# A two-layer decoder trunk on one core: the opening's products of c on 128 rows, four modulations moved to ScalarE, other durations in the instruction planner

## The chip, the cores and the metric

The kernel runs on one core of a Trainium2 chip. The time is that of one execution on the device in microseconds (us). Differences are told by several executions of each kernel on the same chip; the profile is that of one more execution. PE is TensorE (its weight loads are shown as PEld), DVE is VectorE, ACT is ScalarE, POOL is GpSimd and SP is SyncE, which issues most transfers.

## The reference

The kernel computes a decoder trunk of two layers on 256 tokens of width 1024, in float32. Each layer is a half feed-forward step, a token mixer and another half feed-forward step. Each sub-layer normalizes x and modulates it with a shift, a scale and a gate that come from a vector c:

```python
c_act = silu(c)
for layer in range(2):
    sh1, sc1, g1, sh2, sc2, g2, sh3, sc3, g3 = split(c_act @ ada_w[layer] + ada_b[layer], 9)
    h = modulate(rms_norm(x, norm_g[layer, 0]), sh1, sc1)          # h * (1 + sc) + sh
    x = x + 0.5 * g1 * swiglu(h, w_gate[layer, 0], w_up[layer, 0], w_down[layer, 0])   # 1024 -> 2816 -> 1024
    h = modulate(rms_norm(x, norm_g[layer, 1]), sh2, sc2)
    mix = moba_attention(h, ...) if layer == 0 else mla_attention(h, ..., shared_k, shared_v)
    x = x + g2 * mix
    h = modulate(rms_norm(x, norm_g[layer, 2]), sh3, sc3)
    x = x + 0.5 * g3 * swiglu(h, w_gate[layer, 1], w_up[layer, 1], w_down[layer, 1])
```

The second layer's mixer (MLA) makes its queries through a latent of 384 columns, and its shared keys and values through a latent of 256 columns, from x normalized and modulated a second time with a shift and scale of their own (`kv`). There are 16 heads of 64 + 32 columns.

## The kernel before

*Products.* A product of float32 accuracy is made of three: each operand is split into a high part of reduced precision (fp32r) and the rest, and PE adds hi x hi, lo x hi and hi x lo (L774 to L776; in the feed-forward's down-projections and elsewhere L979 and L987). Weights stream in through SP's queue into three raw buffers; ACT rounds them (hi, L644) and DVE subtracts (lo, L645). Activations that leave PSUM are split likewise: ACT hi (L789), DVE lo (L790). The score and value products of the attention (L1043, L1048, L1103) are whole float32 products, with the mask added by a bf16 product (L1044). Transposes are made on PE (L824, L1083, L1410, L1475).

*Who sets the order.* The program is written with delays between its parts, but what stands in each engine's queue in the end is set by a planner (class `Order`). It records every instruction, gives each a duration by a formula (`duration()`, L205 to L250), adds costs such as `SWITCH` for PE's passing to a slow float32 product, places the instructions of every engine one after another with a priority by what is due when, several times over, keeps the best plan, and fixes this order on every engine. A change of a duration formula so reorders instructions of all engines anywhere in the program, without any of them being other work. Instructions inside `ranked(n)` are placed early, in order of n.

*The opening* (`first()`). c is loaded as 32 rows of 256, runs through Silu on ACT twice (L1562 rounded, L1563 whole) and is split. Eight products with a column of the identity broadcast as weights (`row_r`, L1568, 32 rows) spread c over all 128 partitions, four from the high part and four from the rest, into two PSUM tiles; ACT copies them to `c_b` (L1571, two copies of 512 columns). The adaLN columns of the first norm are then made on DVE, for each of 8 steps k: two products with c_b summed along the row (L655, 1024 columns each, for shift and scale), then the scale becomes (1 + scale) x gain (`scale_col`, L660). x is transposed on PE together with its normalization (L1603; from k = 2 on, ACT normalizes, L1607, and PE transposes, L1608). ACT modulates (z, L1620, 256 columns), and z is split into h (ACT L789, DVE L790). The first feed-forward weights of each step are rounded and split (whi, ACT L1631; wlo, DVE L1632) as they land, and 36 products (L1640 to L1642) add into six PSUM accumulators. These are opened by products of zeros (L1579): one each, and two for the accumulators 1 to 3, nine in all; ten more (L1610) fill the wait after the first transposes.

*The second mixer's entry.* When a row tile t of x (128 rows; there are two) is done, `norm_T` and `modulate_cols` make four pieces of 256 columns (c0 = 0, 256, 512, 768): ACT scales x by its norm (y, L819), PE transposes two blocks (L824), and each block is modulated for the mixer's own h and for the `kv` path. The `kv` modulations (z) are on DVE (L840); those of h are on ACT (L842), but those with c0 of 512 and more, where there are two uses, are on DVE too. `split_h` then splits each. `mla()` follows with the latent products of both tiles (L774 to L776, with 384 columns for queries and 288 for keys and values), the latents' norm (L1400 to L1405), their transposes and splits (qlT and ckT, L1410, L789, L790), the up-projections, the head norms and rotations, and four groups of heads: scores, mask, maximum (DVE L1057), exponentials (ACT L1068), transposes of the result (L1083, copied by ACT L1085) and value products (L1103).

## Time and profile before

| what | us |
|---|---|
| median of three executions | 994.26 |
| lowest and highest | 993.56, 994.35 |
| the profiled execution, its own time | 993.19 |
| its span in the profile | 990.8 |

The profiled execution's mean TensorE clock was 0.999 of full speed. A row of a single engine's timeline gives the start, the time, the engine, the line, the operation, what it writes and reads, shapes and a count of neighbours of one kind, and in brackets how long the engine was idle before it and what ended this. A matmul's time in these rows reaches from its start to its end and overlaps with the next one's; the distance of two starts is what one costs. A line such as L1640 is one of the kernel before.

### The profile page before, as it was taken

What the parts mean: (1) busy time and instruction counts of PE and PEld (TensorE: products, weight loads), DVE (VectorE), ACT (ScalarE), POOL (GpSimd) and SP (SyncE); (2) the same over time, 40 slices, a digit from 0 to 9 for tenths busy, and PEclk for the clock granted to TensorE, in tenths of its full rate; (3) what the DMA queues carried; (4) which work ended last, traced back from release to release, by engine and by line L of the source; (5) the groups of instructions that cost most, each with busy time, mean ns of one, the idle gap of its engine ahead of it and who ended that gap; (6) DMA issues with size and microseconds to landing.
All of it is one profiled execution on the core that took longest, in us unless ns stands there. A gap on an engine that the chain in (4) does not pass through costs nothing.

```text
span 990.8 us, 15241 instructions
## 1 busy us (share of the span) xinstructions
PE 979.4 (99%) x5565; PEld 832.1 (84%) x5565; DVE 845.8 (85%) x1431; ACT 629.2 (64%) x1176; POOL 85.6 (9%) x120
## 2 busy tenths in 40 slices
PE   8999999999999999999999999999999999999998
PEld 7988888888887788888888888888888878888886
DVE  7999999898999899999798999974899789677542
ACT  5699565378666966555377665633869796666421
POOL 1012100022131000000010000000143110000000
PEclk9999999999999999999999999999999999999999
DMA  9978989898777678989889988872333568545630
GB/s 367 409 268 280 348 304 370 290 362 304 270 282 259 240 291 317 324 305 347 299 312 323 329 315 335 286 287 88 107 112 128 213 241 300 182 170 175 228 128 21
DMA packets 53274, 260.55 MB, mean 263 GB/s; under 512 B 6192, under 2 KB 6736, under 8 KB 35024
## 3 DMA queue, kind: packets, MB, share of 16 engines
q1 hardware_dynamic: 51696, 255.93, 70.8%
q0 software_dynamic: 1024, 3.17, 1.1%
q8 instruction: 43, 0.70, 0.3%
q10 hardware_dynamic: 480, 0.49, 0.2%
q14 instruction: 31, 0.25, 0.1%
HBM read 255.37 MB, written 4.19 MB: 262 GB/s over the span
## 4 chain that ended last, share of the span: by engine, by line
PE 93%; DVE 3%; DMA 2%; ACT 1%; issue 1%; POOL 0%; ACTq 0%; SPq 0%
PE mm L979 26%; PE mm L774 15%; PE mm L775 15%; PE mm L776 15%; PE mm L987 13%; DMA raw<-in_first_dram 2%; PE at L1103 1%; PE at L1083 1%; PE at L1043 1%; PE tr L1204 1%; PE tr L824 1%; PE tr L1475 1%; PE at L1048 1%; DVE wlo L1632 1%; DVE adaw L655 1%
## 5 line engine op out<-in xcount | busy, mean ns | idle before, releaser
L645 DVE TENSOR_TENSOR lo<-raw,hi 128x1024 fp32r<-128x1024 f32 (+3 forms) x312 | 369.7, 1200 | 69.2 <-ACT hi L644 63.7
L644 ACT ACTIVATE hi<-raw 128x1024 fp32r<-128x1024 f32 (+3 forms) x312 | 320.8, 1038 | 152.5 <-PE mm L776 115.9
L979 PE MATMUL mm<-h,hi 128*128 128x512 f32 x1120 | 288.6, 394 | 0.0
L979 PEld LDWEIGHTS mm<-h,hi 128*128 128x128 f32 x1120 | 199.6, 189 | 34.4
L987 PEld LDWEIGHTS mm<-h,lo 128*128 128x128 f32 x1120 | 155.5, 190 | 12.1
L987 PE MATMUL mm<-h,lo 128*128 128x256 f32 x1120 | 162.3, 283 | 0.0
L655 DVE CUSTOM_DVE_ANT_0 adaw<-adaw,c_b,cols 128x1024 f32<-128x1024 f32 x112 | 141.5, 1278 | 3.0 <-ACT c_b L1571 1.8
L774 PE MATMUL mm<-hi,gh 128*128 128x512 f32 x352 | 137.5, 390 | 0.0
L775 PE MATMUL mm<-lo,gh 128*128 128x512 f32 x352 | 137.2, 390 | 0.0
L776 PE MATMUL mm<-hi,gl 128*128 128x512 f32 x352 | 137.2, 390 | 0.0
L774 PE MATMUL mm<-hi,h 128*128 128x512 f32 (+1 forms) x240 | 95.2, 401 | 0.4 <-ACT h L789 0.3
L776 PE MATMUL mm<-hi,h 128*128 128x512 f32 (+1 forms) x240 | 92.6, 392 | 1.0 <-DVE h L790 1.0
L775 PE MATMUL mm<-lo,h 128*128 128x512 f32 (+1 forms) x240 | 93.0, 391 | 0.0
L776 PEld LDWEIGHTS mm<-hi,gl 128*128 128x128 f32 x352 | 66.1, 188 | 13.9
L775 PEld LDWEIGHTS mm<-lo,gh 128*128 128x128 f32 x352 | 66.1, 188 | 13.3
L774 PEld LDWEIGHTS mm<-hi,gh 128*128 128x128 f32 x352 | 66.1, 188 | 13.3
L693 DVE SCALAR_TENSOR_TENSOR acc<-adaw,cols,acc 128x1024 f32<-128x1024 f32 x48 | 61.3, 1278 | 0.2
L774 PEld LDWEIGHTS mm<-hi,h 128*128 128x128 f32 x240 | 45.1, 188 | 10.2 <-issue 1.3
L776 PEld LDWEIGHTS mm<-hi,h 128*128 128x128 f32 x240 | 45.1, 188 | 10.1 <-DVE h L790 1.2
L775 PEld LDWEIGHTS mm<-lo,h 128*128 128x128 f32 x240 | 45.2, 188 | 7.8
L811 POOL TENSOR_TENSOR rstd<-ssq,mhalf 128x1 f32<-128x1 f32 x12 | 13.5, 1125 | 411.0 <-DVE ssq L806 344.0
L916 ACT ACTIVATE u<-mm 128x256 f32<-128x256 f32 x70 | 26.4, 377 | 34.8 <-PE mm L987 33.6
(240 smaller groups left out, 1246.7 us busy)
## 6 DMA issues: line engine op xcount, KB each, us to landing
raw<-in_w_dram SPq DMA_DIRECT2D x142, 1024.0 KB, 5.4
adaw<-in_ada_dram SPq DMA_DIRECT2D x160, 512.0 KB, 5.5
raw<-in_w_dram SPq DMA_DIRECT2D x12, 512.0 KB, 3.5
raw<-in_first_dram SPq DMA_DIRECT2D x7, 512.0 KB, 9.0
raw<-in_w_dram SPq DMA_DIRECT2D x6, 576.0 KB, 3.7
bias_d<-bt SPq DMA_DIRECT2D x12, 256.0 KB, 3.9
bg<-bias_d POOLq DMA_DIRECT2D x4, 768.0 KB, 6.2
raw<-in_first_dram SPq DMA_DIRECT2D x10, 256.0 KB, 9.0
```

What stands on the lines that cost most here:

```text
L644: nc.scalar.activation(hi, src, AF.Copy)
L645: nc.vector.tensor_tensor(lo, src, hi.bitcast(F32), op=ALU.subtract)
L655: nc.vector.tensor_tensor_reduce(wt, wt, c_b, 1.0, cols[:, i, c:c + 1], op0=ALU.mult, op1=ALU.add, accum_out=m_cols[:, i, c:c + 1])
L693: nc.vector.scalar_tensor_tensor(acc, ada_tile(j, k), cact[:, k:k + 1], acc, op0=ALU.mult, op1=ALU.add)
L774: nc.tensor.matmul(ps, lh, rh, start=start, stop=False)
L775: nc.tensor.matmul(ps, lh, rl, start=False, stop=False)
L776: nc.tensor.matmul(ps, ll, rh, start=False, stop=stop)
L811: nc.gpsimd.tensor_tensor(r, stats[t], mhalf[:, 0:1], op=ALU.pow)
L824: nc.tensor.transpose(kslice(pt, j), kslice(y, j), ident)
L916: nc.scalar.activation(x, ps[:, S:], AF.Copy)
L979: nc.tensor.matmul(ps[i], w[0], hs[2], start=k == 0, stop=False)
L987: nc.tensor.matmul(ps[i][:, S:], w, hk_, start=False, stop=k == KD - 1)
```

## The change

It has three parts.

1. *The planner's figures.* A DVE tensor_scalar with two pointer operands (the modulation) is given 267 + 1.05 n ns instead of 205 + 0.54 n. PE's change of kind is given 95 into a float32 product, 140 (`BACK`) out of one, and -80 (`T_TO_R`) from a transpose to another product. A chain that keeps neighbouring value products together holds the products of c together as well.
2. *The opening.* c's two parts are whole tiles of 128 rows whose rows 32 to 127 are cleared by four memsets on DVE; `row_r` has 128 rows, so c's products run over 128 rows. c's transfer is issued first. One half of `c_b` is copied by ACT, the other by DVE. The accumulators 1 to 3 are opened by four products of zeros each instead of two (15 in all). The scale becomes (1 + scale) x gain on ACT (one column, Identity with scale and bias) and no longer on DVE. In step 0, ACT writes h's high part straight from the transposed x, DVE writes z from it as well, and DVE subtracts; the other steps keep z on ACT and the split.
3. *The second mixer's entry.* For the second row tile (t = 1) the modulations of h with c0 of 512 and more go to ACT: four of 128 columns.

```diff
+BACK = 140.0
+T_TO_R = -80.0
...
+            elif len(aps) > 3 and not full:
+                d = 267.0 + 1.05 * n if n > 8 else d
...
-            half = type(i).__name__ == "InstMatmult" and aps[0].ap[0][1] == DH
+            half = type(i).__name__ == "InstMatmult" and (aps[0].ap[0][1] == DH or aps[1].ap[-1][0] == 0)
...
-                slow = self.ins[k].ins[0].dtype == F32 and not self.ins[k].is_transpose
-                if slow and not dtype:
-                    occ, dur = occ + SWITCH, dur + SWITCH
-                dtype = slow
+                kind = ("transpose" if self.ins[k].is_transpose else
+                        "slow" if self.ins[k].ins[0].dtype == F32 else "product")
+                d = (SWITCH if kind == "slow" and dtype != "slow" else 0.0 if kind == "slow" else
+                     BACK if dtype == "slow" else
+                     T_TO_R if dtype == "transpose" and kind == "product" else 0.0)
+                occ, dur = occ + d, dur + d
+                dtype = kind
...
-                    modulate(pt[:, c:c + step], z[:, c:c + step], key, (c0 + c) // P, step,
-                             on_vector=i > 0 or len(keys) > 1 and c0 >= 512)
+                    modulate(pt[:, c:c + step], z[:, c:c + step], key, (c0 + c) // P, P,
+                             on_vector=i > 0 or len(keys) > 1 and t == 0 and c0 >= 512)
...
-            c4, chi, clo = [tp.tile([P, S], x, tag="y", name=nm("c"), bufs=4)[:32] for x in (F32, F32R, F32R)]
-            row_r = fp.tile([32, 4], F32R, name="row_r")
-            nc.vector.tensor_copy(row_r, ident[:32, :4])
+            c4, chi, clo = [tp.tile([P, S], x, tag="y", name=nm("c"), bufs=4) for x in (F32, F32R, F32R)]
+            with ranked(0):
+                nc.scalar.dma_start(c4[:32], a["c"])
+                for x in (chi, clo):
+                    for p in (32, 64):
+                        nc.vector.memset(x[p:2 * p].bitcast(F32), 0.0)
+            row_r = fp.tile([P, 4], F32R, name="row_r")
+            nc.vector.tensor_copy(row_r, ident[:, :4])
...
-                for i in range(2):
-                    nc.scalar.activation(c_b[:, i * 512:(i + 1) * 512], pc[i], AF.Copy)
+                nc.scalar.activation(c_b[:, :512], pc[0], AF.Copy)
+                nc.vector.tensor_copy(c_b[:, 512:], pc[1])
...
-                for i in range(2 if 1 <= f < 4 else 1):
+                for i in range(4 if 1 <= f < 4 else 1):
...
-                    scale_col(key, k, 1)
+                    g = col_slice(2, key, k, 1)
+                    nc.scalar.activation(col_slice(1, key, k, 1), col_slice(1, key, k, 1), AF.Identity, scale=g, bias=g)
...
-                    nc.scalar.activation(z, xT[k], AF.Identity, scale=col_slice(1, key, k, 1), bias=col_slice(0, key, k, 1))
...
-                    split_evac(hh, hl, z)
+                    if k:
+                        modulate(xT[k], z, key, k, S)
+                        split_evac(hh, hl, z)
+                    else:
+                        modulate(xT[k], hh, key, k, S)
+                        modulate(xT[k], z, key, k, S, on_vector=True)
+                        nc.vector.tensor_tensor(hl, z, hh.bitcast(F32), op=ALU.subtract)
```

The queues of SP and POOL keep their order. PE's, DVE's and ACT's change in some sixty stretches, since the planner sees other costs; most of them lie in the opening, in the mixers (207 to 360 and 699 to 819 us of the profile before) and at 514 to 531 us.

More of the change, by code (lines that the diff above doesn't have):

```diff
@@ L836, in modulate @@
     def modulate(xT, z, key, k0, n, on_vector=False):
-        for j in range(n // P):
+        for j in range(xT.shape[-1] // n):
+            js = slice(j * n, (j + 1) * n)
             shift, scale = [col_slice(i, key, k0 + j, 1) for i in range(2)]
             if on_vector:
-                nc.vector.tensor_scalar(kslice(z, j), kslice(xT, j), scale, shift, op0=ALU.mult, op1=ALU.add)
+                nc.vector.tensor_scalar(z[:, js], xT[:, js], scale, shift, op0=ALU.mult, op1=ALU.add)
             else:
-                nc.scalar.activation(kslice(z, j), kslice(xT, j), AF.Identity,
-                        scale=scale, bias=shift)
+                nc.scalar.activation(z[:, js], xT[:, js], AF.Identity, scale=scale, bias=shift)
     def split_h(h, c0, n, z):
```

9 lines of the change are left out of this document (4 added, 5 removed).

## The prediction

> **What bounds the kernel now.** I read the page first, then the chain of waits for the opening, then what PE waits for around the second mixer's entry, and last the rows of single engines there.
>
> ```profile
> span 990.8 us, 15241 instructions
> ...
> PE 979.4 (99%) x5565; PEld 832.1 (84%) x5565; DVE 845.8 (85%) x1431; ACT 629.2 (64%) x1176; POOL 85.6 (9%) x120
> ...
> PE 93%; DVE 3%; DMA 2%; ACT 1%; issue 1%; POOL 0%; ACTq 0%; SPq 0%
> ```
>
> PE sets the end: 93% of the chain. The change takes away no product of the layers, so it can only win where PE waits: in the opening (the chain's share of DVE, DMA and ACT), and at the second mixer's entry. The time of this profiled execution is 993.19 us, 1.07 below the median of 994.26; I make the sum as a difference against the profiled execution and add it to the median.
>
> The chain of waits over the first 60 us (start, length, what) shows the opening:
>
> ```profile
> 44.80 0.57 ACT z L1620
> 45.40 0.43 ACT h L789
> ```
>
> From 45.83 on (45.40 and 0.43) PE has all it needs of the first layer, so whatever the opening wins must show as an earlier z of the last of its eight steps.
>
> What PE waits for from 695 to 735 us (total, times, longest):
>
> ```profile
> PE mm L776 <- DVE h L790: 1.0, 1, 1.0
> PE mm L774 <- ACT ckT L789: 0.8, 1, 0.8
> PE mm L774 <- ACT qlT L789: 0.6, 1, 0.6
> PE mm L776 <- DVE qlT L790: 0.3, 1, 0.3
> PE mm L775 <- DVE lo L645: 0.2, 1, 0.2
> ```
>
> These five waits are 2.9 us of idle time. A wait costs PE some 0.2 more than that, because products else overlap (by 0.16: 787.88 and 0.40 against 788.12, in the rows under (e)) and the first one behind it is slow; so 3.9 us is all that the second part can win there. The stretches in which they lie (columns: window, length, busy PE, PEld, DVE, ACT, POOL with counts, clock, DMA share, GB/s):
>
> ```profile
> 700.00:710.00 10.00, 8.85 (x55) 8.04 (x54) 9.73 (x26) 8.64 (x24) 1.00 (x1) 1.00 0.34 101
> 710.00:720.00 10.00, 9.58 (x62) 8.68 (x61) 9.55 (x28) 7.55 (x23) 3.25 (x4) 1.00 0.13 47
> 740.00:750.00 10.00, 10.00 (x81) 8.27 (x80) 9.58 (x21) 9.23 (x28) 2.59 (x2) 1.00 0.41 140
> ```
>
> DVE is the full engine there (9.73 of 10), but ACT has only 1.36 us free in the first stretch and 2.45 in the second.
>
> **Part one, the opening.** The rows of ACT, DVE and PE (start, length, line, what, count, idle before and its releaser):
>
> ```profile
> 6.61 1.08 ACT L1571 ACTIVATE c_b<-tr 128x512 f32<-128x512 f32 x2 [2.20 <-PE tr L1568]
> ...
> 43.05 1.59 ACT L1631 ACTIVATE whi<-raw 128x1024 fp32r<-128x1024 f32 x2 [1.82 <-DMA raw<-in_first_dram]
> 44.80 0.56 ACT L1620 ACTIVATE z<-tr,m_cols 128x256 f32<-128x256 f32 x1 [0.16 <-DVE m_cols L660]
> ```
> ```profile
> 7.80 1.28 DVE L655 CUSTOM_DVE_ANT_0 adaw<-adaw,c_b,cols 128x1024 f32<-128x1024 f32 x1 [1.80 <-ACT c_b L1571]
> ...
> 44.62 0.15 DVE L660 SCALAR_TENSOR_TENSOR m_cols<-m_cols,cols 128x1 f32<-128x1 f32 x1
> ```
> ```profile
> 1.00 3.17 PE L1579 MATMUL mm<-zeros 128*128 128x512 bf16 x7 [1.00 <-DVE zeros L1528]
> 4.09 1.22 PE L1568 MATMUL tr<-c,row_r 32*128 32x256 f32 x4
> ```
>
> ```profile
> 0.83 0.11 DVE L1528 MEMSET zeros<- 128x64 uint32 x1 [0.83 <-PEq L1682]
> ...
> 0.93 0.17 DVE L619 MEMSET ones_r<- 128x128 f32 x1
> ```
>
> *Head.* Of the four new memsets three stand on DVE ahead of the one that clears zeros, which PE waits for until 1.00. They clear 256 columns each; the nearest row clears 128 in 0.17, so I take 0.2 us each, 0.6 in all (bounds 0 and 1). Then seven zeros products of 3.17 us end near 4.75 instead of 4.17, and the products of c start some 0.55 later than 4.09. Their price of 1.22 for four is kept: the columns streamed are the same. Against that, one zeros product that stood between the two halves of c's products (0.5 us) moves behind them, and the second copy of c_b goes to DVE: the two copies take 1.08 one after the other, so side by side half of it, 0.5, goes. Sum: +0.6 - 0.5 - 0.5, with a wait between engines more; the first column of DVE starts at 7.8 or up to half a us earlier. The six more zeros products (6 x 0.45 = 2.7 us at the pitch of the seven) stand behind c's products, where PE waits for x and c_b in any case until 9.31.
>
> *Body and end.* What is won at the head doesn't reach the end. The last raw tile lands at 43.03 (whi waits 1.82 us for it and starts at 43.05); ACT then rounds it in two pieces of 1.59 us together, to 44.64; z stands behind these and starts at 44.80, 0.16 later, because the scale L660 on DVE ends at 44.77. If L660 goes, z can start at 44.64 at the earliest, unless it is put ahead of the rounding; but the step that takes its place on ACT (one column, some 0.1 between neighbours) stands in the same row behind the first piece. In the changed order ACT does: one piece, the scale, the other piece, z, h. So z starts at 44.70 to 44.75. **Value: -0.1 us**, bounds 0 (the scale costs ACT what DVE saved) and -0.16. Only if the transfers land earlier could it be more, and their order on SP is unchanged:
>
> ```profile
> 30.00:40.00 10.00, 9.93 (x85) 9.72 (x84) 10.00 (x17) 6.87 (x12) 0.00 (x0) 1.00 1.03 405
> ```
>
> the DMA engines are full (1.03) at 405 GB/s, so an earlier free buffer brings no tile sooner. The first step's side by side h (ACT) and z (DVE) saves one pass of some 0.5 us there, at 11 us, well ahead of these landings: nothing at the end.
>
> *A page on the 128 rows.* The seven zeros products are 0.45 us apart for 512 columns, while products of that width are 0.24 apart later (788.12 after 787.88 below): PE begins at half its rate although the clock column says 1.00. The Trainium skill, page "TensorE: Matmul & The Clock Gate", section "Part 1: The HAM clock gate", has PE at half rate until a window of about 3.4 us was busy; the section "Why this matters for your kernels" says that a single product on 32 rows takes the time of one on 128. By the second, 128 rows win nothing in themselves; by the first, an unbroken run of full products could end the half rate earlier, which would halve the 2.4 us of c's products at most. The trace shows no case of this, and by the landing at 43.03 the end would stand all the same.
>
> **Part two, the second mixer's entry.**
>
> ```profile
> 700.59 0.72 DVE L840 TENSOR_SCALAR y<-tr,m_cols 128x128 f32<-128x128 f32 x2
> 701.23 0.41 DVE L790 TENSOR_TENSOR h<-y,h 128x256 fp32r<-128x256 f32 x1
> ...
> 702.68 1.36 DVE L840 TENSOR_SCALAR z<-tr,m_cols 128x128 f32<-128x128 f32 x4
> 703.96 1.04 DVE L645 TENSOR_TENSOR lo<-raw,hi 128x864 fp32r<-128x864 f32 x1
> ```
> ```profile
> 701.70 0.44 PE L776 MATMUL mm<-hi,h 128*128 128x384 f32 x1 [0.96 <-DVE h L790]
> ...
> 705.06 0.40 PE L775 MATMUL mm<-lo,hkv 128*128 128x288 f32 x1 [0.18 <-DVE lo L645]
> ```
> ```profile
> L842 ACT ACTIVATE y<-tr,m_cols x72: 433/447/462, 208.1 to 813.0; 128x128 f32<-128x128 f32 x72
> ```
>
> DVE's modulations come 0.32 us apart (four from 702.68 to 703.96). The four that move are those of the second row tile (c0 of 512 and more): 4 x 0.32 = 1.28 us less on DVE, and 4 x 0.4 = 1.6 us more on ACT (0.447 each alone, less when pipelined).
>
> (a) They lie behind 705, so the *first* wait isn't touched by them; but the new durations reorder DVE. Between the residual's end and the split that PE waits for at 701.70 stand three modulations instead of two, one more at 0.32: **+0.3**.
>
> (b) The split lo of the kv weights (703.96, PE waits for it at 705.06) goes behind six z modulations and a split of hkv, at (a)'s 0.3 later, and ends near 706.2 instead of 705.0. PE resumes there at 706.3: **+1.2** in all, (a) among it. Two transposes of y, which wait for y of L819 and so for a split of hkv, stand at the same place.
>
> (c) From there DVE is 1.28 us lighter, and the second tile's h comes at some 706.4 instead of 707.0. The later waits, for qlT (0.6 and 0.3) and ckT (0.8), cost 1.7 + 3 x 0.2 = 2.3, and I take them as gone: +1.2 - 2.3 = -1.1 near 725. Behind that, the weight split for the next products has DVE's column of moved splits ahead of it; I take half of its 1.04 us as a new wait, which leaves **0.5 us ahead** at 733. The bounds of (b) and (c) together are -3.9 (no wait left) and +1.2 (the later waits stay).
>
> (d) What follows takes it back. The attention's first scores stand behind this, and their exponentials fill ACT:
>
> ```profile
> 738.42 0.37 ACT L1068 ACTIVATE s<-at,mx 128x128 f32<-128x128 f32 x1 [1.35 <-DVE mx L1057]
> ...
> 743.88 1.59 ACT L1085 ACTIVATE pT<-at 128x512 f32<-128x512 f32 x3
> ```
>
> ACT runs almost without a pause from 738.42 to 745.4 (9.23 busy of the 10 us from 740), and PE's transposes wait for it. In the new order the first mask product comes behind one score more (0.43 us), so it is 0.5 - 0.43 = 0.07 earlier: of the 0.5 us ahead, 0.07 is left at 745.
>
> (e) PE's order is changed in many places, since the planner's prices of switches differ. Whether a switch costs is seen here:
>
> ```profile
> 785.47 0.63 PE L774 MATMUL mm<-hi,h 128*128 128x512 f32 x2
> 786.03 1.58 PE L1103 MATMUL at<-pT,v 128*64 128x128 f32 x24
> 787.54 0.50 PE L776 MATMUL mm<-hi,h 128*128 128x512 f32 x1
> 787.88 0.40 PE L774 MATMUL mm<-hi,h 128*128 128x512 f32 x1
> 788.12 0.40 PE L775 MATMUL mm<-lo,h 128*128 128x512 f32 x1
> ```
> ```profile
> 779.26 0.39 PE L774 MATMUL mm<-hi,h 128*128 128x512 f32 x1
> 779.49 1.03 PE L1043 MATMUL at<-kT,qT 96*128 96x256 f32 x4
> 780.36 0.27 PE L1044 MATMUL at<-mask,ident_b 128*128 128x256 bf16 x1
> ```
>
> Out of the products with 64 wide weights (L1103) the first follower takes 0.34 instead of 0.24 (787.54 to 787.88), and into them there is the same 0.1 (785.47 to 786.03 is 0.56 for two that take 0.47); with the first and last of the 64 wide ones slower by as much, a way there and back is some 0.4 us. Into the scores (L1043) it is 0.23, nothing. The changed order puts one product of the next weights amid the first head group's L1103, a way there and back more: **+0.4**, bounds 0 (hidden in the wait for the next pT there) and 0.5. The other new switches are scores and transposes, at nothing; if a restart's 0.2 applied to each of four of them, 0.8 more.
>
> Sum of part two: -0.07 + 0.4 = **+0.3**. DVE's truer durations reorder the rest too (46 to 700 and 800 to 991 us), but PE runs there without a wait for another engine to speak of; I take 0, with 0.5 either way.
>
> **Total:** -0.1 + 0.3 = +0.2 us, 993.4 for the profiled execution, 994.5 for the median. A measurement of this kernel can tell about 0.2% (2 us) from no change; so this is no change.
>
> **Rivals.**
>
> *A, faster: the entry's waits go for good.* For: DVE is the full engine of that stretch, 1.28 us leaves it, and three of the five waits are behind the point where it leaves. If all goes, 3.9 us at the entry and 0.16 at the opening, and ACT's run of exponentials starts as much earlier: 994.26 - 4.0 = 990.2. The likelier half: the later three waits (2.3) are kept through (d) and (a) and (b) cost nothing, 992.0. Against: the three waits would have to end with no new one, and (d) ties PE to ACT.
>
> *B, slower: ACT becomes the bound of the entry.* Four modulations of 0.4 are 1.6 us on an engine with 1.36 free from 700 to 710. It decides if ACT has them ahead of what PE needs next (h's hi halves, hi of the next weights): then the waits are no shorter, and the 1.6 us comes on top, with (a) at 0.3 and (e) at 0.4: +2.3, 996.6. With the rest of (b), 0.9, not regained either, 997.5. Against: 2.45 us are free in the stretch behind, and the modulations of one tile stand alone between splits.
>
> *C, the opening doesn't do what it says:* the head's win ends at the transfer of 43.03, and the end moves by 0 to 0.16. That is part of the forecast. The other way is that the head is late: c_b 0.6 us later would be taken up by the 1.82 us that ACT has ahead of the last landing, and DVE's own row (10.00 of 10 busy from 30 to 40) would carry it to the end: +0.6, 994.9, still no change.
>
> **How the numbers follow.** Forecast with C (within 2 us): 0.70. A: 0.12, faster by over 0.2%. B: 0.18, slower by over 0.2%, with what of (b) and (e) adds up to as much. The range leaves out 1 in 10 at each side: from the likelier half of A, 992.0, to just past B's first price, 996.8; the unknown costs (opening -0.16 to +0.6, L1103's way 0 to 0.5 and the other switches to 0.8, the rest 0.5 either way) lie inside.
>
> **What would show it.** Right: z of the last step at 44.7 with whi still at 43.05; PE's first wait at the entry growing from 0.96 to some 1.2 us, the second from 0.18 to over 1 us, and those for qlT and ckT gone or under 0.3 each; ACT's first exponential within 0.3 us of 738.42. Wrong: the last raw landing earlier than 43.03 (then the opening gives more); kv's lo split ending by 705.5 (then A); ACT over 9.5 of 10 busy from 700 to 710 and PE's waits there naming ACT (then B).

## The result and the profile after

| | us |
|---|---|
| before: median of 22 executions (lowest, highest) | 994.15 (992.78, 996.40) |
| after: median of 22 executions (lowest, highest) | 995.44 (994.12, 997.18) |
| after over before, 95% interval | 1.0013 [1.0007, 1.0019] |
| after's profiled execution, its span | 994.84, 993.1 |

The change costs 1.3 us (0.7 to 1.9). By the forecast's bound of 0.2% that is no change, and 995.44 lies in its range; but its sum was +0.2, and the question is where the 1.3 us come from. On after's page, span, engines and chain:

```profile
span 993.1 us, 15264 instructions
...
PE 978.1 (98%) x5568; PEld 830.1 (84%) x5571; DVE 847.5 (85%) x1425; ACT 631.8 (64%) x1186; POOL 82.7 (8%) x120
...
PE 91%; DMA 3%; DVE 3%; ACT 2%; issue 1%; SPq 0%; POOL 0%; ACTq 0%; DVEq 0%
```

PE is 1.3 us less busy than before and the span is 2.3 us longer: the loss is waiting. The profiles show more of it than the medians, since both of before (spans of 990.8 and 990.9) are among its shortest executions: 15 timed beside the second have a median span of 992.2 and a lowest of 990.7, while after's two (993.1 and 993.3) stand near the median of 993.7 of its 22. To place it I take the start of the same products in both traces and subtract (PE's starts; "entry" is the first score product of the first mixer, 239.50 before):

| kernel, one profile each | first FFN product (50.22) | entry of the first mixer (239.50) | second FFN resumes (824.02) | last product ends (986.00) |
|---|---|---|---|---|
| after | +0.21 | +2.68 | +2.36 | +2.36 |
| after, profiled again | +0.11 | +2.91 | +2.62 | +2.62 |
| before, profiled again | +0.19 | +0.11 | +0.10 | +0.10 |

So between 50 and 239.50 us PE loses 2.5 us in one profile and 2.8 in the other. Behind that 0.3 come back, 0.2 of it in the second mixer, which I had taken for the main scene. What PE waits for in after from 100 to 230 us (total, times, longest):

```profile
PE tr L831 <- ACT y L826: 0.6, 1, 0.6
PE mm L987 <- DVE u L925: 0.2, 1, 0.2
PE mm L783 <- DVE h L797: 0.2, 1, 0.2
```

The same view of before has no line at all. The first and the third of these waits are at 214 to 217 us, and PE's rows there show both:

```profile
215.11 0.50 PE L783 MATMUL mm<-hi,h 128*128 128x512 f32 x1 [0.21 <-DVE h L797]
...
217.15 0.44 PE L831 MATMUL tr<-ident,y 128*128 128x128 f32 x2 [0.59 <-ACT y L826]
```

Each costs more than its idle time (the product behind a pause is slow): PE's starts fall back by 0.38 us at the first and by 0.78 at the second, 1.17 in all. Of the rest, 0.8 us is lost ahead of them (after is +0.21 at 50.22 and +1.03 from 140 to 206 us), and some 0.5 in pieces of about 0.1 up to 239.50, at the products behind the two pauses and at transposes, where the rows name no wait. The experiments tell the parts apart.

At the second mixer's entry after's waits from 695 to 735 us are these:

```profile
PE mm L783 <- DVE h L797: 1.2, 1, 1.2
PE tr L831 <- ACT y L826: 1.0, 1, 1.0
PE mm L781 <- ACT ckT L796: 0.5, 1, 0.5
PE mm L781 <- ACT qlT L796: 0.4, 1, 0.4
PE mm L782 <- DVE lo L652: 0.3, 1, 0.3
```

They are 3.4 us against 2.9, and still the stretch doesn't end later: over the whole second mixer after is 2.54 us late at the start and 2.36 at the end. Which of the restarts and passings between kinds of products pays for the difference, these rows don't tell.

### The profile page after: what moved, and what is told of

It reads as the page before. It is cut to its first block, busy times and chain, and to the rows that moved or that the text cites. A ratio compares the mean times of both kernels' runs of the same rounds, so it can differ in the third digit from the quotient of the medians.

```text
span 993.1 us, 15264 instructions
## 1 busy us (share of the span) xinstructions
PE 978.1 (98%) x5568; PEld 830.1 (84%) x5571; DVE 847.5 (85%) x1425; ACT 631.8 (64%) x1186; POOL 82.7 (8%) x120
## 3 DMA queue, kind: packets, MB, share of 16 engines
q0 software_dynamic: 1024, 3.17, 1.1%
## 4 chain that ended last, share of the span: by engine, by line
PE 91%; DMA 3%; DVE 3%; ACT 2%; issue 1%; SPq 0%; POOL 0%; ACTq 0%; DVEq 0%
PE mm L987 26%; PE mm L781 15%; PE mm L782 15%; PE mm L783 15%; PE mm L995 13%; DMA raw<-in_first_dram 3%; PE at L1111 1%; PE at L1091 1%; PE at L1051 1%; PE tr L1212 1%; PE tr L831 1%; PE at L1056 1%; DMA raw<-in_w_dram 1%; DVE adaw L662 1%; DVE lo L652 1%
## 5 line engine op out<-in xcount | busy, mean ns | idle before, releaser
L700 DVE SCALAR_TENSOR_TENSOR acc<-adaw,cols,acc 128x1024 f32<-128x1024 f32 x48 | 61.8, 1287 | 0.1
```

The lines of the kernel that those rows point to most:

```text
L700: nc.vector.scalar_tensor_tensor(acc, ada_tile(j, k), cact[:, k:k + 1], acc, op0=ALU.mult, op1=ALU.add)
```

## The experiments

**Theory 1**: the replanned order (the planner's new durations) costs PE time at the first mixer's entry, and the moved modulations themselves win. **Rival**: the opening's products on 128 rows or its copies shift the landing of the weights, and what is lost later follows from that. Each part was run alone first, then two of them together, these four on one chip (before: 993.39 there). "Measured" gives the median in us, the ratio to before on the same chip with its 95% interval, and what the profile shows; +2.47 means 2.47 us later than in before's first profile.

### The planner's figures alone

```diff
+BACK = 140.0
+T_TO_R = -80.0
...
+            elif len(aps) > 3 and not full:
+                d = 267.0 + 1.05 * n if n > 8 else d
```

and the three kinds of PE in the planner, on the kernel before; no instruction's work differs.

> The kernel before with the planner's three figures alone (the price of DVE's modulation, 140 out of a float32 product, -80 from a transpose to a product): no opening, no modulation moved. My theory: the losses at the second mixer's entry and behind it belong to these figures, since DVE's order there then puts the kv weights' lo split behind six z modulations and PE's order has two more switches to 64-wide products, as in the changed kernel; so PE's first wait there grows from 0.96 us and the second from 0.18 to about 1, and the total is 0.5 to 1 us above before. The waits at 214 to 217 us, which the changed kernel has and before has not, should be absent, because here only one accumulation stands ahead of the norm's sum of squares on DVE; z of the opening's last step at 44.80. Rival (the moved modulations burden ACT): the entry is as in before, the total the same within 0.3 us.

Measured: 994.54, 1.0009 [1.0000, 1.0019]. The profile is +2.47 at the first mixer's entry and +2.18 at the end. PE waits 1.1 and 0.3 us at 116 to 123 us, for DVE's g and u, which come late from a late tile (below), and not at 214 to 217 us. The first two waits at the second mixer are 1.2 and 1.0 as expected, but the mixer as a whole wins 0.17 (2.35 at its start, 2.18 at the end): the total came out near the expected one, not where the theory had the loss.

### The opening alone

```diff
-            row_r = fp.tile([32, 4], F32R, name="row_r")
+            row_r = fp.tile([P, 4], F32R, name="row_r")
...
-                for i in range(2 if 1 <= f < 4 else 1):
+                for i in range(4 if 1 <= f < 4 else 1):
...
-                    scale_col(key, k, 1)
+                    g = col_slice(2, key, k, 1)
+                    nc.scalar.activation(col_slice(1, key, k, 1), col_slice(1, key, k, 1), AF.Identity, scale=g, bias=g)
```

and the rest of the change's second part.

> The kernel before with the new opening alone. My theory: z of the last step starts at 44.9 to 45.0 (0.2 later, as in the changed kernel), nothing else is lost: one accumulation goes behind the sum of squares, so the waits at 214 to 217 us are as small as in before; total +0.2 us, within 0.5. Rival (the opening itself, through its shifted transfers, costs what the changed kernel loses by 217 us): waits of 1.6 us there and a total of +1.3 to +2 us.

Measured: 995.39, 1.0022 [1.0012, 1.0031], the largest loss of the parts, and as large as the rival had it. But it is not lost in the opening (+0.33 at its end): the profile is +2.19 at the first mixer's entry, where PE's starts fall back three times (by 0.30 at 209.02, 0.51 at 216.74 and 0.27 at 217.80), and +3.26 behind the first mixer; +2.82 is left at the end. The opening's instructions enter the plan, so the order changes hundreds of microseconds behind them.

### The four modulations alone

```diff
-                             on_vector=i > 0 or len(keys) > 1 and c0 >= 512)
+                             on_vector=i > 0 or len(keys) > 1 and t == 0 and c0 >= 512)
```

> The kernel before with the four modulations moved to ACT alone. My theory: the kv weights' lo split stays where it was, PE's first two waits of the entry stay at 0.96 and 0.18 us, the later ones (for qlT and ckT, 0.6, 0.3 and 0.8 us) fall by 1 us or more together, and what is won there is kept but for what ACT's exponentials take: total 0.5 to 1.5 us below before. Rival (ACT becomes the bound of the entry): PE waits for ACT between 700 and 715 us, and the total is 1 us or more above before.

Measured: 993.68, 0.9998 [0.9988, 1.0007]; lowest 991.12 where before's lowest is 992.25. Its profile is +2.43 at 700 us and +1.24 at the end: the second mixer wins 1.2 us, although the median is not the expected 0.5 to 1.5 us below before. Its waits from 695 to 735 us show why:

```profile
PE mm L776 <- DVE h L790: 1.0, 1, 1.0
...
PE mm L775 <- DVE lo L645: 0.2, 1, 0.2
```

The first wait stays at 1.0 and kv's split is not delayed (0.2): with the old durations the planner leaves the split at its place. After loses most of this gain again by its own figures.

### Opening and modulations, without the figures

Both edits above on the kernel before.

> The opening and the moved modulations without the planner's figures. My theory: the sum of the two alone, so 0.3 to 1.3 us below before, and 1.5 to 2.5 us below the changed kernel; no waits of over 0.3 us at 214 to 217 us, since there too one accumulation stands behind the sum of squares. Rival (opening and modulations cost, the figures help): at or above the changed kernel's time, 1.3 us above before.

Measured: 994.51, 1.0005 [0.9996, 1.0014]; +3.44 before the second mixer, which wins 1.5, and +1.95 at the end. PE's starts fall back near the first mixer's entry again (by 0.30 at 209.73 and 0.73 at 218.35; idle 0.13 and 0.57) without any figure changed, though for other things than in after: the second is for a weight split (lo, L645). So theory 1 is too narrow: not the figures as such, but any plan in which the opening differs can lose time there.

### Each kernel again

> The kernel before once more, for a second profile. The run with the moved modulations alone has the same order on every engine up to 700 us as before, and yet reached the first mixer 2.4 us later than before's profile. My theory: an execution of the same program varies by that much there, since DVE is full from 46 to 217 us and every late transfer that stops ACT or DVE comes back as a wait of PE at 116 to 123 us or 204 to 217 us; before's profile was an execution with none. So this profile shows PE waits of 0.5 to 2 us at 116 to 123 us and a span of 991.5 to 993. Rival (before has no such waits, the changes make them): no PE wait over 0.3 us between 100 and 217 us, first score product at 239.5 within 0.4.

> The changed kernel once more. My theory: z of the last opening step again at 45.0, and the waits at 214 to 217 us (0.3 and 0.6 us idle) again, as they come from DVE's order; the sum of PE's waits from 100 to 217 us differs from the first profile by up to 1.5 us. Rival (all of it is chance): waits of under 0.3 us at 214 to 217 us.

Before gave 992.62 (span 990.9) and no wait from 100 to 230 us, neither at 116 to 123 nor at 214 to 217: the rival was right. After gave 995.10 (993.3) and the same two waits at 214 to 217 us, as expected.

### One accumulation moved back

After's order, read at this place, has DVE make one more step of the gate's column (L700) before the sum of squares (L813), and ACT's split of that column, two more splits and then y follow in one queue. DVE and ACT of after and, in the second fence, of before:

```profile
204.52 2.60 DVE L700 SCALAR_TENSOR_TENSOR acc<-adaw,cols,acc 128x1024 f32<-128x1024 f32 x2
207.03 0.75 DVE L813 CUSTOM_DVE_ANT_0 ry<-x,ssq 128x512 f32<-128x512 f32 x1
...
207.20 1.06 ACT L651 ACTIVATE hi<-acc 128x1024 fp32r<-128x1024 f32 x1 [3.63 <-DVE acc L700]
...
216.60 0.50 ACT L826 ACTIVATE y<-x,rstd 128x256 f32<-128x256 f32 x1
```
```profile
203.49 1.28 DVE L693 SCALAR_TENSOR_TENSOR acc<-adaw,cols,acc 128x1024 f32<-128x1024 f32 x1
204.68 0.75 DVE L806 CUSTOM_DVE_ANT_0 ry<-x,ssq 128x512 f32<-128x512 f32 x1
...
213.93 0.51 ACT L819 ACTIVATE y<-x,rstd 128x256 f32<-128x256 f32 x1
```

**Theory 2**: that one step, 1.28 us on DVE, delays y. **Rival**: ACT's queue does. The kernel is after with just these two neighbours exchanged in DVE's order:

```diff
+        ks = order["DVE"]
+        p = next(p for p, k in enumerate(ks) if self.ins[k].name in squares)
...
+        ks[p - 1], ks[p] = ks[p], ks[p - 1]
```

> The changed kernel with one instruction of DVE moved: the second of the two gate accumulations that stand ahead of the first mixer's sum of squares goes behind it, everything else in its place. My theory (the two accumulations delay the norm by 1.2 us and make PE's waits there): the sum of squares starts at some 205.8 instead of 207.0, the waits at 214 to 217 us shrink from 1.5 us of lost time to 0.5 or less, total 1 us below the changed kernel, so +0.0 to +0.5 us against before. Rival (DVE is full there and late in any case): the waits move to the accumulation's user or stay, total as the changed kernel, +1 to +2 us.

Measured: 995.57, 1.0015 [1.0006, 1.0024]. The sum of squares is early, and y is later:

```profile
206.01 0.74 DVE L821 CUSTOM_DVE_ANT_0 ry<-x,ssq 128x512 f32<-128x512 f32 x1
206.68 1.28 DVE L707 SCALAR_TENSOR_TENSOR acc<-adaw,cols,acc 128x1024 f32<-128x1024 f32 x1
...
208.04 1.06 ACT L657 ACTIVATE hi<-acc 128x1024 fp32r<-128x1024 f32 x1 [4.56 <-DVE acc L707]
...
217.11 0.50 ACT L834 ACTIVATE y<-x,rstd 128x256 f32<-128x256 f32 x1
```

ACT's split of the column stands ahead of y in ACT's queue; it now waits 4.56 us instead of 3.63, and PE's waits at 214 to 217 us are as they were (0.2 and 0.6), with one of 0.2 for y at 210.50 more. Theory 2 falls: the column has to be whole before its split, in whatever order DVE makes its last steps, and y follows that split in ACT's queue.

### c's products on 32 rows again

After with

```diff
-                        nc.tensor.matmul(pc[k // 2][:, k % 2 * S:(k % 2 + 1) * S], row_r[:, k:k + 1].to_broadcast([P, P]), x,
+                        nc.tensor.matmul(pc[k // 2][:, k % 2 * S:(k % 2 + 1) * S], row_r[:32, k:k + 1].to_broadcast([32, P]), x[:32],
```

This changes the planner's order as well.

> The changed kernel with c's products on 32 rows of the same tiles. If 128 active rows end PE's half rate at 5 us in the changed kernel, the products of c are 0.3 us apart again for 256 columns and the zeros behind them 0.43 for 512, the full rate comes behind 10 us, and c_b is copied 0.8 us later; z of the last step still starts at 45.0 within 0.3, since DVE's steps of 4.6 us and the landing of the raw tiles set it. Rival (the unbroken run of zeros ends the half rate, not the rows): the same pitches as in the changed kernel, 0.12 to 0.16.

> The changed kernel with c's products on 32 rows, timed now: its single profile had no PE wait between 46 and 700 us and a span 2.1 us below the changed kernel's. My theory (weight tiles that land about 2 us late near 95 us, in some executions, decide; the rows don't): the median stands near the changed kernel's, +0.5 to +1.5 us against before, and its fastest run is within 0.5 us of 993. Rival (128 rows, by the earlier full rate of PE, shift the first layer's transfers so that they are late always): a median of -0.5 to +0.5 us against before, 1 us below the changed kernel's.

A single execution gave 992.96; timed, the same kernel gave 994.36, 1.0001 [0.9992, 1.0011], with a profile of span 993.0 where the first had 991.2. In the first, c's products on 32 rows are 0.12 apart from 4.74 us on, so on the half rate the rival was right. The first profile has no wait at 214 to 217 us and is +0.44 at the end. In the second DVE waits 0.7 us near 204 us for an adaLN tile that lands late, and PE 0.6 for y at 209 us. So one program in one order differs by 1.8 us in span, and its ratio is that of no change where after's interval begins at 1.0007. That is the number of the rival, by which the 32 rows themselves help; since the order differs too, the next runs had to tell.

### 32 rows in the kernel without figures

The same line on top of opening and modulations.

> The opening with c's products on 32 rows and the four moved modulations, without the planner's figures. If the rows matter as the rival above has it and the moved modulations win 1.2 us at the second mixer as their own run showed: 1 us or more below before, the fastest version. If executions with late tiles decide and the opening costs 0.2 to 1 us: within 0.5 us of before, as the same with 128 rows (+0.5).

Measured: 995.71, 1.0009 [1.0000, 1.0017], +3.19 at the first mixer's entry, more than either expectation. 32 rows are no gain in themselves: with this plan the kernel is no faster than with 128.

### The modulations alone, again

> The moved modulations alone once more, to halve the interval of the first (-0.2 us, -1.2 to +0.7). My theory: the second mixer takes 1.2 us less, the rest is unchanged in order, so 0.5 to 1.5 us below before in the median. Rival (what is won there is lost elsewhere): within 0.3 us of before. The profile again tells whether tiles landed late in the first layer: without them the first score product of the first mixer starts at 239.5 to 239.7, as in both profiles of before.

Measured: 994.02, 0.9993 [0.9983, 1.0003]; lowest 991.54, before's beside it 992.62. The second mixer wins 1.1 us (+2.70 to +1.62); the interval holds the theory's 0.5 to 1.5 us and the rival's 0.3. The first score product starts at 242.12, so the tile landed late here too.

### 32 rows in exactly after's order

The planner is told 128 rows, so that every engine keeps after's order, and the products run on 32:

```diff
-                    p1 = p0 + ap.ap[0][1]
+                    p1 = p0 + (P if kind == "InstMatmult" and ap.ap[0][1] == 32 else ap.ap[0][1])
```

> The changed kernel with c's products on 32 rows and with exactly the changed kernel's order on every engine (the run before with 32 rows had an order of its own). It tells the rows from the order. If the rows matter (the earlier full rate of PE makes the first layer's tiles land late always): a median within 0.5 us of before's and a fastest run near 992.6, as in the 32 rows' own order. If the changed kernel's order is what costs: median +1 to +2 us against before, fastest run at 994 or above, and the waits of 0.3 and 0.6 us at 214 to 217 us again, with the full rate of PE later than in the changed kernel or not. The opening's z stands at 45.0 within 0.2 either way.

Measured: 995.68, 1.0010 [0.9999, 1.0021]. Its waits from 46 to 330 us:

```profile
PE mm L987 <- DVE g L925: 2.1, 1, 2.1
PE tr L831 <- ACT y L826: 0.6, 1, 0.6
PE mm L987 <- DVE u L925: 0.2, 1, 0.2
PE mm L783 <- DVE h L797: 0.2, 1, 0.2
```

The last three lines are after's, to the tenth, with 32 rows. This kernel and the one with 32 rows in its own order hold the same instructions; they differ in the order alone, and only this one has the waits at 214 to 217 us. **What follows**: the waits at 214 to 217 us belong to the order, not to the rows. The interval holds 1, so the median does not tell it; the trace does, and so does the lowest execution (994.50, before's 992.64; in the 32 rows' own order it was 992.55, before's 992.62).

### All profiles side by side: what the order costs

DVE is full there and on PE's way. Three marks, as differences to before's profile: ACT's last weight split ahead of the gate column's (released by PE: 202.50 after, 201.47 before), DVE's split of that column, and PE at the first mixer's entry. Here are ACT and DVE of after, then of before:

```profile
202.50 1.06 ACT L651 ACTIVATE hi<-raw 128x1024 fp32r<-128x1024 f32 x1 [1.66 <-PE mm L783]
...
208.84 1.22 DVE L652 TENSOR_TENSOR lo<-acc,hi 128x1024 fp32r<-128x1024 f32 x1
```
```profile
201.47 1.06 ACT L644 ACTIVATE hi<-raw 128x1024 fp32r<-128x1024 f32 x1 [1.66 <-PE mm L776]
...
206.49 1.22 DVE L645 TENSOR_TENSOR lo<-acc,hi 128x1024 fp32r<-128x1024 f32 x1
```

| kernel | ACT at 201.47 | DVE at 206.49 | added between | PE at 239.50 |
|---|---|---|---|---|
| before again | +0.17 | +0.17 | 0 | +0.11 |
| figures alone | +2.38 | +2.38 | 0 | +2.47 |
| modulations alone, and again | +2.43, +2.68 | +2.44, +2.68 | 0, 0 | +2.39, +2.62 |
| 32 rows, one execution | +0.38 | +0.39 | 0 | +0.50 |
| 32 rows, timed | +0.89 | +1.68 | 0.8 (late adaLN tile) | +1.78 |
| opening alone | +1.09 | +2.11 | 1.0 | +2.19 |
| opening and modulations | +1.81 | +2.82 | 1.0 | +2.76 |
| the same with 32 rows | +2.91 | +4.33 | 1.4 | +3.19 |
| after, and again | +1.03, +1.26 | +2.35, +2.57 | 1.3, 1.3 | +2.68, +2.91 |
| after, two steps exchanged | +0.95 | +2.64 | 1.7 | +3.17 |
| after's order, 32 rows | +3.17 | +4.55 | 1.4 | +4.84 |

Save for one kernel, PE is as late at 239.50 as DVE at the split, to 0.6 us and mostly to 0.1. In after's order PE is 0.3 to 0.5 later than DVE, the small pieces named above. So there are two losses. What stands in the first column is gathered ahead of it and differs between executions. What is added between is 0 in every profile in which the planner left this stretch as in before, 1.0 to 1.4 in the plans with the opening's edit and without the figures, and 1.3 to 1.7 in after's.

The lowest executions split the kernels the same way without any profile. Against before's lowest beside them, those with nothing added by their order are at -0.1 (figures alone), -1.1 and -1.1 (modulations alone, which win that much at the second mixer) and -0.1 (32 rows, timed). Those with 1.0 to 1.7 added are at +1.3 (after), +1.8 (two steps exchanged), +1.9 (after's order, 32 rows), +2.8 (opening alone), +1.8 (opening and modulations) and +1.9 (the same with 32 rows). After's own set apart (22 each), these are 11 or 12 executions against 15 to 35 of before, so that before's lowest is a little favoured.

For after's order the rows name it. The gate's column has eight steps of 1.28 us on DVE, and the order decides how many of them are done before DVE's last long pause ahead of the split, the wait for ACT's hi at 191 to 193 us. Before has made three by then; five are left (192.94, 195.55, two from 198.27, 203.49). After has made two; six are left (193.97, two from 196.58, 200.24, two from 204.52). One step is 1.28 us, and 1.3 is what is added. The kernel with 32 rows, where nothing is added, has five left as well. DVE's pause in before and, in the second fence, in after; before has no other over 0.3 us from 175 to 205 us, while after has three more, of 1.50 (182.58), 0.71 (188.20, for the square of x, ry, which stands later in ACT's queue) and 0.54 (203.18):

```profile
191.73 1.23 DVE L645 TENSOR_TENSOR lo<-raw,hi 128x1024 fp32r<-128x1024 f32 x1 [2.97 <-ACT hi L644]
```
```profile
192.77 1.22 DVE L652 TENSOR_TENSOR lo<-raw,hi 128x1024 fp32r<-128x1024 f32 x1 [1.88 <-ACT hi L651]
```

That also says why the exchange of two steps changed nothing: six were still left. Putting a third step back ahead of the pause was not tried, so the cause is read from rows that agree in place and size in four profiles, and not isolated. In the three plans of the opening without the figures five steps are left, and the time goes with another place of the order: ACT's first y stands ahead of its split of the column there, and DVE waits for this split (0.81, 0.81 and 1.22 us idle, where before has no such wait).

### What is lost ahead of that: a late tile

The kernel with the modulations alone keeps before's order on every engine up to 700 us, and yet its profiles are 2.4 and 2.7 us late by 201 us. At 95 us its ACT row (first fence) stands against before's (second):

```profile
97.11 1.06 ACT L644 ACTIVATE hi<-raw 128x1024 fp32r<-128x1024 f32 x1 [1.77 <-DMA raw<-in_w_dram]
```
```profile
95.30 2.02 ACT L644 ACTIVATE hi<-raw 128x1024 fp32r<-128x1024 f32 x2
```

The tile lands at 97.09 where before's profile has 94.49, though it was issued earlier (89.58 against 89.67). The delay reaches PE through DVE. Before's window from 80 us (window, length, busy PE, PEld, DVE, ACT, POOL, clock, DMA, GB/s):

```profile
80.00:100.00 20.00, 20.00 (x174) 17.25 (x173) 19.13 (x28) 18.39 (x39) 5.37 (x4) 1.00 0.83 291
```

With 19.13 and, in the next 20 us, 19.93 of 20 busy, DVE can't make up 2 us, and twenty microseconds later PE waits for g. PE of the kernel with the modulations alone:

```profile
118.17 2.56 PE L980 MATMUL mm<-h,hi 128*128 128x512 f32 x10 [1.04 <-DVE g L918]
```

Up to there the instructions and their order are before's, so this looks like a matter of the execution and not of the change. It is not shown: the figures alone, with before's order up to 207 us, have such a tile too (96.39), so that three profiles of two changed kernels have it and the two of before (94.49 and 94.44) do not. That the changed kernels also run without the loss, their lowest executions say (991.12, 991.54 and 992.14, as far below before's as their second mixers win). That before's longer executions have it is my reading of their spread (992.25 to 996.34 in 35 executions); none of them is profiled. After has such a tile in both profiles (96.30 and 96.17), and loses 0.7 and 1.0 us by 140 us. The 2.1 us for g in the last experiment follow another late transfer: ACT waits 2.26 us, until 79.94, for a store of bt. What makes transfers land late is open.

## Why the prediction was right or wrong

**The total.** No change within 0.2%: right. The sum of +0.2 was near by luck: both of its terms came out with the other sign (opening -0.1 forecast, +0.1 to 0.2 measured; second mixer +0.3 forecast, -0.2 measured), and the term that costs most was put at 0. On PE's rows after's two profiles show +0.2 and +0.1 up to 50.22, +0.1 by 100 us, +1.65 from 201 to 239.50 (one step of the gate's column on DVE, 1.3, felt at the two waits as 0.38 and 0.78, and the small pieces), and -0.3 from there to the end. Together that is +1.6, inside the measured 0.7 to 1.9; the lowest executions, 992.78 before and 994.12 after, differ by 1.3. The late tile (0.7 and 1.0) is left out of this sum. That is a choice and not shown: the modulations alone have it in both profiles at a median near before's, but no execution of before that has it was profiled.

**The step that failed** is "DVE's truer durations reorder the rest too ... I take 0, with 0.5 either way". PE ran there without a wait *in before's order*; that says nothing of the cover in the new one. Ahead of the first mixer the new order leaves DVE one step of 1.28 us more to do in the stretch where it is full and PE waits for it: 1.65 us on PE's rows by 239.50. The bound of 0.5 came from no row. The row to take was this step's own, and the place could be read off the two orders, which I had done for the second mixer only.

**The opening: -0.1 forecast, +0.1 to 0.2 measured.** The head's seven zeros products start at 1.99 and not 1.00 (+1.0, the upper bound; 0.6 taken), c's products at 4.59 against 4.09 (0.55 forecast). The landing held (whi at 43.05 again, and so nothing won at the head reached the end: right). The tile that I called the last to land is the last but one; the last lands at 43.61, still ahead of its rounding at 44.02, so the argument stands. But z starts at 45.00 in after, and not at 44.70 to 44.75. That alone is within the spread, since before's second profile has 44.98. Counted from the start of whi, which follows the landing, it is clear: 1.75 to 1.84 us in four profiles with the old opening (one more, with 2.47, is held up elsewhere), 1.94 to 2.03 in all nine with the new one. After's ACT rows:

```profile
43.05 1.07 ACT L1649 ACTIVATE whi<-raw 128x1024 fp32r<-128x1024 f32 x1 [1.61 <-DMA raw<-in_first_dram]
44.01 0.37 ACT L1631 ACTIVATE m_cols<-m_cols,cols 128x1 f32<-128x1 f32 x1
44.29 0.62 ACT L1649 ACTIVATE whi<-raw 128x512 fp32r<-128x512 f32 x1
```

The one-column scale that I priced at "some 0.1 between neighbours" takes 0.37, and the piece of whi behind it starts 0.28 later. The Trainium skill, page "ScalarE: Activation LUTs", section "Rules for kernel authors", gives an activation with a pointer for its bias some 0.3 us besides the time of its elements; this row agrees. By these rows z could start when the piece of whi is done, at 44.91 (44.29 and 0.62) at the latest. But after's chain of waits shows another engine that ends as late, and names that one:

```profile
30.57 0.14 ACT m_cols L1631
...
43.70 1.20 DVE adaw L662
45.00 0.57 ACT z L851
```

In step 3 the scale, between two pieces of whi, makes z 0.26 later than before (31.28 against 31.02 in ACT's rows; the chain cuts overlaps off). DVE waits for the h that follows and hands the delay down to its last column. One row of DVE in after, and the same of before:

```profile
32.30 0.42 DVE L797 TENSOR_TENSOR h<-z,h 128x256 fp32r<-128x256 f32 x1 [0.47 <-ACT h L796]
```
```profile
32.07 0.42 DVE L790 TENSOR_TENSOR h<-z,h 128x256 fp32r<-128x256 f32 x1
```

So the last z waits for DVE's column (43.70 and 1.20: 44.90). Rival C had this path ("DVE's own row would carry it to the end") with another cause.

**The 128 rows and the half rate: the rows as forecast, the rate in part.** After's PE rows (first fence), those of after's order with 32 rows (second) and those of before, profiled again (third):

```profile
4.59 1.42 PE L1580 MATMUL tr<-c,row_r 128*128 128x256 f32 x8
...
10.46 0.72 PE L1622 MATMUL tr<-zeros 128*128 128x128 bf16 x10
```
```profile
5.09 1.57 PE L1580 MATMUL tr<-c,row_r 32*128 32x256 f32 x8
...
10.62 0.72 PE L1622 MATMUL tr<-zeros 128*128 128x128 bf16 x10
```
```profile
4.38 0.83 PE L1568 MATMUL tr<-c,row_r 32*128 32x256 f32 x4 [0.22 <-ACT c L1562]
...
11.02 1.27 PE L1610 MATMUL tr<-zeros 128*128 128x128 bf16 x10
```

Eight products take 1.42 us on 128 rows and 1.57 on 32, where the first three still run at half rate; at full rate both are 0.12 apart, so the rows win nothing. The ten fill products take 0.72 in both kernels whose zeros follow on c's products without a break, and 1.27 in both profiles of before, where PE has stood idle in between. So the unbroken run holds the full rate. The Trainium skill's page "TensorE: Matmul & The Clock Gate", "Part 1: The HAM clock gate", with its busy window of some 3.4 us, had led me to expect that the half rate also ends earlier. That is not shown: before's second profile is at full rate from 4.7 us on, after from 5.0, and before loses it again. The first layer product starts 1.1 us earlier in after (11.07 against 12.21), and nothing of that is left at 43.05.

**The second mixer: +0.3 forecast, -0.2 measured**, step by step:

- (a) The first wait is 1.2 us: right.
- (b) PE loses 1.4 and 1.2 us at its first two waits, where before loses 1.2 and 0.4: 1.1 more, against 1.2 forecast. The second shows as 1.0 for y and not as kv's split: both stand at that place, as said, and y ends last.
- (c) The forecast's own figures give 0.6 ahead at 733 (1.1 less half of 1.04), not 0.5. Measured are 0.9 us ahead near 725 against 1.1 forecast (the last transposes of the latents are +1.65 where the stretch began at +2.54; what stands ahead of them differs in the two orders), then a new wait of 0.3 for a split (0.5 forecast). The waits for qlT and ckT are 0.4 and 0.5, not "under 0.3 each": that mark was wrong, the sum right.
- (d) The first exponential is at 740.72, and so 0.24 ahead instead of 0.07, inside the mark of 0.3.
- (e) PE in the first group of value products, after and then before:

```profile
746.97 0.44 PE L1111 MATMUL at<-pT,v 128*64 128x128 f32 x4
747.34 0.51 PE L781 MATMUL mm<-hi,ckT 128*128 128x512 f32 x1
747.78 1.36 PE L1111 MATMUL at<-pT,v 128*64 128x128 f32 x20
749.07 2.24 PE L1051 MATMUL at<-kT,qT 96*128 96x128 f32 x12
```
```profile
744.66 1.74 PE L1103 MATMUL at<-pT,v 128*64 128x128 f32 x24
746.33 1.16 PE L1043 MATMUL at<-kT,qT 96*128 96x128 f32 x8
```

From the first value product to the scores behind them it is 2.10 us against 1.67. Of the 0.43 more, 0.23 is the product of weights itself, which is only moved; the way there and back costs 0.2, half of my 0.4. With (d) that is 0.4 of the 0.5 us by which this part was off. The passing out of the scores, which I had put at nothing, does cost: the first product behind them, at 737.69, is 0.37 ahead of the next, and those that follow 0.17.

**The rivals.** A fell: the waits stay in sum. Yet its mechanism is real: with the modulations alone the second mixer wins 1.1 to 1.2 us; after's figures take 1.0 of it. The four modulations with the opening and without the figures win 1.5. B fell: ACT is busy 8.75 of 10 us from 700 to 710, under the 9.5 that I had named, and 8.68 in the 10 us from 702.5. Half of its sign is there, though: PE's wait of 1.0 us names ACT (y).

**A better version.** The modulations alone (0.9998 and 0.9993, up to 1.0007 and 1.0003) are below after (from 1.0007 on), but both intervals hold 1, so they are not shown to beat before; their lowest executions, 991.12 and 991.54, are 1.1 us below before's beside them, as much as the second mixer wins in their profiles.

## What to carry to other kernels

Where a planner sets the order, an edit of a few instructions or of a price is an edit of the whole order: read the new order at every place where a full engine feeds PE closely, and count there how much of that engine's work is left behind its last pause, not only where the edit is. "No wait in this stretch" describes the old order and is no cover for the new one. And price a moved one-column step by the engine that it moves to: it is its fixed cost, in the row of the busiest queue, that counts.

## What the hardware showed beside that

- One kernel in one order spreads by some 2 us of span (991.2 and 993.0), and a tile that landed at 94.49 in before landed at 97.09 in a kernel with the same order up to there; DVE behind it, busy 39.06 of the 40 us from 80 to 120 in before, has no free time to make it up.
- The half rate at the start differs from one execution of a kernel to the next: before ran at it until 13 us in one profile; in the other it was at full rate from 4.7 us on and at half rate again from 8.7, after pauses of 0.5 and 1.7 us.
- Passing between kinds of products can cost PE 0.1 us or more. A rounded product of 512 columns is 0.23 us ahead of the next of its kind. In before it is 0.32 ahead of value products with weights 64 wide, and the first one behind these is 0.34 ahead of the next (six times each); the whole float32 scores on 64 rows give the same two figures (four times each). Into the scores on 96 rows it cost nothing (0.23 us from 779.26 to 779.49); out of them the first product took 0.1 and 0.2 more in after's two cases.
- In the opening a one-column step takes 0.37 to 0.39 us on ACT, and the next instruction starts 0.27 to 0.29 behind it between neighbours; on DVE it takes 0.15, and the next starts 0.07 behind it.
